# The second feed-forward product in Strassen's form, and lower parts of weights by an accumulating load, in a two-layer encoder trunk

## The chip, the cores and the metric

The kernel runs on one core of one Trainium2 chip. The metric is the device time of one execution in microseconds (us), as a median over runs; smaller is better.

## What is computed

Two layers, each with attention, a recurrent branch and a feed-forward block, over 768 tokens (512 and 256 in two groups) of 1024 features. The change touches the feed-forward block alone:

```python
def encoder_layer(x, l, ...):
...
    x = x + merged @ w_out
    h2 = rmsnorm(x, norm2_g)
    return x + jnp.square(jax.nn.relu(h2 @ w_ff1)) @ w_ff2     # w_ff1 1024 x 4096, w_ff2 4096 x 1024, fp32
```

## The kernel before, in words

**Precision.** Every fp32 operand is split into an upper part (`hi`, rounded to the fp32r type of the matmul) and a lower part `lo = x - hi`. A product is three matmuls: hi x hi, hi x lo, lo x hi. `split` (L203 to L209) makes the two: ACT copies the upper part (L206), DVE subtracts (L209).

**Weights.** `plan` lists every weight tile of 128 x 1024 in the order of use. `wload` (L274) hands out the next and has `prefetch` (L257) prepare the one eight places on: SP loads it into a buffer `raw` or `rw`, ACT and DVE split it into `whi` and `wlo`, of which there are four buffers each. Every engine works in order on its own instructions. PE's order is that of the code; a scheduler sets that of ACT, DVE, POOL and SP.

**Feed-forward.** The 4096 hidden features go in 8 chunks of 512 (L963 on). The features on the partitions are the contraction; tokens are the free dimension, in two halves `TS[0]`, `TS[1]` of 384. In a chunk:

- FF1, `h2 @ w_ff1`, is in the Strassen-Winograd form, seven products q over quarters (two halves of the features, two halves of tokens). Of its weights a1, a2 and b2 are quarters as loaded, P1 to P4 are sums of quarters, made by `ff_operand` on DVE (L235 to L255). A strip is twelve matmuls (4 blocks of the contraction, three each) into a PSUM tile of 128 x 384. `FP` gives the order of the 14 strips as pairs (p, q), p the half of the hidden features. Strips with equal b accumulate in the same tile (L987), `bank[p, b]`.
- After certain strips ACT copies out of PSUM (L996, L998, L1003), DVE combines (L1000, L1004, L1009) and `hidden` follows: DVE takes the positive part times the row scale (L973), ACT squares (L974), `split` makes upper and lower part, 384 wide, into `hs`.
- FF2, `... @ w_ff2`, is plain: four weight tiles of two output blocks jj each, two token halves t, twelve matmuls each in `mm3` (L286 to L288), 16 strips, and DVE adds each tile of 128 x 384 to the residual `xt` (L1024).

So a chunk has 14 x 12 + 16 x 12 = 360 matmuls of 384 columns. PSUM for the block has eight tiles of one bank. In the first chunk of a layer the row scale `rb2` itself is computed after strip (1, 6) by `stats` (matmuls L370 and L371, DVE L320 and L323). In the last chunk each finished residual tile is stored.

Of the kernel before, what the change touches and what calls it, by code (L numbers as in the profile page):

```python
# [79 lines left out]
def trunk_kernel(ctx: ExitStack, tc: tile.TileContext, xT, wqk, wv, wx, wy, wg0, wg1, wa, wr, wo, wf1, wf2,  # L80
                 rgw, vec, rep, rot, out):
# [5 lines left out]
    mp = ctx.enter_context(tc.tile_pool(name="mp", bufs=8))  # L87
# [115 lines left out]
    def split(hi, lo, src, eng="act"):  # L203
# [3 lines left out]
        else:  # L207
# [5 lines left out]
          "wf1": wf1, "wf2": wf2, "rgw": rgw}  # L213
    plan, ready = [], []
    for l in range(DEPTH):
# [14 lines left out]
        for c in range(FF // 512):  # L230
            plan += [("wf1", l, c, x) for x in FW] + [("wf2", l, c * 4 + s) for s in range(4)]
# [24 lines left out]

    def prefetch(upto):  # L257
        while len(ready) < min(upto, len(plan)):
            k = plan[len(ready)]
            if k[0] == "wf1":  # L260
                raw, n = ff_operand(*k[1:]), 1024
# [9 lines left out]
            split(hi, lo, raw)  # L271
# [61 lines left out]
    def squares(xt, g, alloc, before=None):  # L333
# [13 lines left out]
        hi, lo = alloc(n, F32R, "s"), alloc(n, F32R, "s")  # L347
# [33 lines left out]
    def slot(tag, dt=F32, w=T):  # L381
        return mp.tile([P, w], dt, tag=tag, name=nm("s" + tag))
# [4 lines left out]
    def norm1(l, xt, alloc):  # L387
# [23 lines left out]
    nTh, nTl, nss = norm1(0, xt, lambda n, dt, s: slot(gx, dt, n) if s == "s" else e0.tile([P, n], dt, tag="e", name=nm(s)))  # L411
    st0.close()

    for l in range(DEPTH):
# [442 lines left out]
        ppf = pool(ffst, f"pf{l}", bufs=8, space=PSUM)  # L857
# [97 lines left out]


        nss = []
        for off, n in GROUPS:
            nss.append([mp.tile([P, n], F32R, tag=gl, name=nm("s")) for i in range(2)])
            split(*nss[-1], sqa[:, off:off + n])  # L960
        rb2 = cp.tile([P, T], F32, tag="rb", name=nm("rb"), bufs=1)
        NC_ = FF // 512
        for c in range(NC_):  # L963
            last = c == NC_ - 1
            hs = {}

            def hidden(s, t, z, r_):

                for i in range(2):
                    if (s, i) not in hs:  # L970
                        hs[s, i] = slot(gl, F32R) if not last else eslot(F32R) if s < 2 else rslot(F32R)
                hi, lo = (hs[s, i][:, TS[t]] for i in range(2))
                V.scalar_tensor_tensor(out=r_, in0=z, scalar=0.0, in1=rb2[:, TS[t]], op0=ALU.max, op1=ALU.mult)  # L973
                S.activation(r_, r_, AF.Square, scale=0.5)  # L974
                split(hi, lo, r_)
# [141 lines left out]
```

## Time and profile before

| | |
|---|---|
| median of 3 runs | 2671.68 us (2670.53 to 2671.82) |
| the profiled execution | 2671.98 us |
| its span (first to last instruction) | 2670.2 us |
| PE busy, matmuls | 2637.9 us (99%), 16456 |
| PE weight loads | 2491.2 us (93%) |
| DVE busy | 1827.0 us (68%) |
| ACT busy | 1414.1 us (53%) |
| POOL busy | 93.8 us (4%) |

A busy share is the share of the span in which the engine executes something; the engines work side by side and wait for each other by semaphores. The feed-forward block is the stretch from about 839 to 1340 us in layer 0 and the last 500 us in layer 1. PE is the matmul engine TensorE, DVE VectorE, ACT ScalarE, POOL GpSimd, SP SyncE, which here issues loads.

### The profile page before, as it was taken

How to read it: one execution, taken by the hardware profiler on the slowest of the kernel's cores; microseconds unless marked ns; L12 is line 12 of the kernel's file. 1: busy time of each engine (PE TensorE's matmuls, PEld its weight loads, DVE VectorE, ACT ScalarE, POOL GpSimd, SP SyncE). 2: the span in 40 equal slices, each digit the busy share in tenths (PEclk: the TensorE clock that was granted, in tenths of full speed). 3: DMA queues.
4: the chain of work that ended last, by engine and by line, in shares of the span. 5: the costliest groups of instructions: out<-in, count | busy, mean ns of one | idle time of the engine just before them, and what ended most of it. 6: DMA issues, size and time to landing. Idle time of an engine off the chain costs nothing.

```text
span 2670.2 us, 40667 instructions
## 1 busy us (share of the span) xinstructions
PE 2637.9 (99%) x16456; PEld 2491.2 (93%) x16456; DVE 1827.0 (68%) x3222; ACT 1414.1 (53%) x2453; POOL 93.8 (4%) x134
## 2 busy tenths in 40 slices
PE   8999999999999999999999999999999999999999
PEld 8999888888889999999999998888888899999999
DVE  8877873698568666555678788737975686555654
ACT  7787872477435333333467878715683363333332
POOL 0000000000020000000100000000001200000000
PEclk9999999999999999999999999999999999999999
DMA  3111114212331221211221111231223321211112
GB/s 133 54 46 53 50 65 144 66 58 71 121 115 64 71 73 64 71 64 56 100 72 52 42 64 38 92 128 55 69 65 122 115 72 64 72 64 64 64 56 79
DMA packets 57484, 199.33 MB, mean 75 GB/s; under 512 B 7504, under 2 KB 10960, under 8 KB 57296
## 3 DMA queue, kind: packets, MB, share of 16 engines
q1 hardware_dynamic: 48384, 161.50, 18.3%
q0 software_dynamic: 8192, 34.61, 3.6%
q8 instruction: 129, 2.11, 0.3%
q10 hardware_dynamic: 720, 0.62, 0.1%
q14 instruction: 59, 0.48, 0.1%
HBM read 177.83 MB, written 18.87 MB: 74 GB/s over the span
## 4 chain that ended last, share of the span: by engine, by line
PE 85%; DVE 7%; ACT 6%; issue 1%; DMA 0%; DVEq 0%; ACTq 0%
PE d L286 13%; PE d L288 13%; PE d L287 13%; PE d L992 6%; PE d L991 6%; PE d L993 6%; PE d L433 4%; PE d L434 4%; PE d L432 4%; PE s L609 3%; PE d L311 2%; PE d L310 2%; PE d L312 2%; PE d L561 2%; PE d L559 2%; PE d L560 2%
## 5 line engine op out<-in xcount | busy, mean ns | idle before, releaser
L206 ACT ACTIVATE whi<-raw 128x1024 fp32r<-128x1024 f32 (+1 forms) x272 | 280.1, 1031 | 455.3 <-PE d L287 277.5
L209 DVE TENSOR_TENSOR wlo<-raw,whi 128x1024 fp32r<-128x1024 f32 (+1 forms) x272 | 330.2, 1216 | 92.0 <-ACT whi L206 89.5
L286 PE MATMUL d<-sZ,whi 128*128 128x384 f32 (+2 forms) x896 | 300.4, 335 | 0.3 <-DVE rec L379 0.3
L287 PE MATMUL d<-sX,whi 128*128 128x384 f32 (+2 forms) x896 | 300.4, 335 | 0.0
L287 PE MATMUL d<-sZ,whi 128*128 128x384 f32 (+2 forms) x896 | 300.4, 335 | 0.0
L288 PE MATMUL d<-sZ,wlo 128*128 128x384 f32 (+2 forms) x896 | 300.2, 335 | 0.0
L286 PEld LDWEIGHTS d<-sZ,whi 128*128 128x128 f32 x896 | 169.1, 189 | 9.4 <-DVE rec L379 0.5
L288 PEld LDWEIGHTS d<-sZ,wlo 128*128 128x128 f32 x896 | 169.1, 189 | 9.0
L287 PEld LDWEIGHTS d<-sZ,whi 128*128 128x128 f32 x896 | 169.1, 189 | 8.8
L287 PEld LDWEIGHTS d<-sX,whi 128*128 128x128 f32 x896 | 169.1, 189 | 8.8
L206 ACT ACTIVATE whi<-ws 128x1024 fp32r<-128x1024 f32 x48 | 50.9, 1061 | 235.5 <-PE d L287 212.8
L286 PE MATMUL d<-sX,whi 128*128 128x384 f32 (+2 forms) x512 | 171.1, 334 | 0.0
L288 PE MATMUL d<-sX,wlo 128*128 128x384 f32 (+2 forms) x512 | 171.1, 334 | 0.0
L432 PE MATMUL d<-whi,sY 128*128 128x256 f32 x512 | 147.8, 289 | 0.0
L432 PE MATMUL d<-whi,sZ 128*128 128x256 f32 x512 | 147.8, 289 | 0.0
L197 ACT ACTIVATE p<-s,nb,sc 128x512 f32<-128x512 f32 (+1 forms) x192 | 134.5, 703 | 21.8 <-DVE nb L612 20.1
L434 PE MATMUL d<-whi,sZ 128*128 128x256 f32 x512 | 145.3, 284 | 0.0
L433 PE MATMUL d<-wlo,sY 128*128 128x256 f32 x512 | 145.2, 284 | 0.0
L434 PE MATMUL d<-whi,sX 128*128 128x256 f32 x512 | 145.2, 284 | 0.0
L433 PE MATMUL d<-wlo,sZ 128*128 128x256 f32 x512 | 145.1, 283 | 0.0
L1024 DVE TENSOR_TENSOR sZ<-sZ,d 128x384 f32<-128x384 f32 x128 | 69.6, 553 | 109.2 <-PE d L288 109.2
L1024 DVE TENSOR_TENSOR sY<-sY,d 128x384 f32<-128x384 f32 x128 | 69.5, 552 | 92.7 <-PE d L288 92.7
(360 smaller groups left out, 7875.7 us busy)
## 6 DMA issues: line engine op xcount, KB each, us to landing
raw<-wf SPq DMA_DIRECT2D x96, 512.0 KB, 3.2
raw<-wqk SPq DMA_DIRECT2D x32, 512.0 KB, 3.4
raw<-wg SPq DMA_DIRECT2D x32, 512.0 KB, 3.3
rw<-wf SPq DMA_DIRECT2D x32, 512.0 KB, 3.3
raw<-wv SPq DMA_DIRECT2D x16, 512.0 KB, 3.8
raw<-wa SPq DMA_DIRECT2D x16, 512.0 KB, 4.5
raw<-wx SPq DMA_DIRECT2D x16, 512.0 KB, 3.2
raw<-wy SPq DMA_DIRECT2D x16, 512.0 KB, 3.2
```

Source lines behind the costliest of these rows:

```text
L206: S.activation(hi, src, AF.Copy)
L209: V.tensor_tensor(out=lo, in0=src, in1=hi.bitcast(F32), op=ALU.subtract)
L286: PE.matmul(ps, lhsT=wh, rhs=xh, start=(k == 0), stop=False)
L287: PE.matmul(ps, lhsT=wh, rhs=xl, start=False, stop=False)
L288: PE.matmul(ps, lhsT=wl, rhs=xh, start=False, stop=(k == n - 1))
L432: PE.matmul(j, lhsT=xh, rhs=hi[:, kk], start=(k == 0), stop=False)
L433: PE.matmul(j, lhsT=xh, rhs=lo[:, kk], start=False, stop=False)
L434: PE.matmul(j, lhsT=xl, rhs=hi[:, kk], start=False, stop=(k == 7))
L991: PE.matmul(ps, lhsT=hi[:, k], rhs=oh, start=new and k == 0, stop=False, skip_group_check=True)
L992: PE.matmul(ps, lhsT=hi[:, k], rhs=ol, start=False, stop=False, skip_group_check=True)
L993: PE.matmul(ps, lhsT=lo[:, k], rhs=oh, start=False, stop=k == 3, skip_group_check=True)
L1024: V.tensor_tensor(out=xg, in0=xg, in1=ps, op=ALU.add)
```

## The change

**FF2 in Strassen's form.** In all chunks but layer 0's last, FF2 takes seven products too, in the order `FP2 = (1, 2, 6, 5, 3, 7, 4)`, each over all four strips r of a quarter of the output (two blocks of 128) before the next product begins. A strip is six matmuls (2 blocks of the contraction), so a chunk has 7 x 4 x 6 = 168 where 192 stood. The weights are a1, a2, b2 and P1 to P4 again (with other signs), made by `ff_operand`. The hidden tiles `b11, b12, b21, b22` (512 features x 768 tokens, as pairs) are summed on DVE and split 768 wide by `h_split` (L209 on ACT, L212 on DVE), seven times a chunk. DVE adds two finished strips at a time into the residual, 128 x 2 x 384 (L1063), 14 times a chunk.

**Lower parts of plain weights.** For a1, a2 and b2 of both products, six a chunk, DVE's subtraction is gone: ACT writes the upper part (L293) and then minus the upper part into `wlo` (L294), and POOL issues a load of the same weights out of DRAM that adds to what stands in `wlo` (L295).

**PSUM and slots.** For chunks there are four PSUM tiles of two banks in place of eight of one bank; the two halves p of FF1, and two strips r of FF2, lie in one tile. The token tiles come in pairs so that two residual blocks are adjacent. Layer 0's last chunk stays plain (`wf2s`), with two blocks jj in one PSUM tile.

```diff
+FP2 = (1, 2, 6, 5, 3, 7, 4)
+FW2 = {1: "a1", 2: "a2", 6: "P2", 5: "P1", 3: "P4", 7: "P3", 4: "b2"}
...
-    mp = ctx.enter_context(tc.tile_pool(name="mp", bufs=8))
+    mp = ctx.enter_context(tc.tile_pool(name="mp", bufs=4))
...
+    def strassen2(l, c):
+        return l + 1 == DEPTH or c + 1 < FF // 512
...
         for c in range(FF // 512):
-            plan += [("wf1", l, c, x) for x in FW] + [("wf2", l, c * 4 + s) for s in range(4)]
+            plan += [("wf1", l, c, x) for x in FW]
+            plan += [("wf2", l, c, FW2[q]) for q in FP2] if strassen2(l, c) else [("wf2s", l, x) for x in range(4)]
...
-            split(hi, lo, raw)
+            if acc is None:
+                split(hi, lo, raw)
+            else:
+                S.activation(hi, raw, AF.Copy)
+                S.activation(lo, hi.bitcast(F32), AF.Copy, scale=-1.0)
+                G.dma_start(out=lo, in_=acc, accum_op=ALU.add)
...
-        ppf = pool(ffst, f"pf{l}", bufs=8, space=PSUM)
+        st = ExitStack()
+        ppf = pool(st, f"pf{l}", bufs=8, space=PSUM)
...
+        st.close()
+        ppf = pool(ffst, f"pff{l}", bufs=4, space=PSUM)
+        def banks():
+            return ppf.tile([P, 2, 512], F32, tag="d", name=nm("d"))
...
-                if new:
-                    bank[p, b] = ppf.tile([P, TH], F32, tag="d", name=nm("d"))
-                ps = bank[p, b]
+                if b not in bank:
+                    bank[b] = banks()
+                ps = bank[b][:, p, 0:TH]
...
+            def h_split(src, late=False):
+                hi, lo = (eslot(F32R), eslot(F32R)) if late else (slot(gl, F32R), slot(gl, F32R))
+                split(hi, lo, src)
+                return [z.rearrange("p (k t) -> p k t", k=2) for z in (hi, lo)]
+            def two(out, u, v, op):
+                V.tensor_tensor(out=out, in0=u, in1=v, op=op)
+            b11, b12, b22, b21 = (hid[x] for x in ("a0", "a1", "b1", "b0"))
+            if str2:
+                o2 = {1: h_split(b11), 2: h_split(b21)}
+                two(b12, b22, b12, ALU.subtract)
+                two(b11, b12, b11, ALU.add)
+                o2[6] = h_split(b11)
+                xb, yb, zb = {}, {}, {}
+                for q in FP2:
+                    if q == 5:
+                        o2[3] = h_split(b22)
+                        two(b22, b22, b11, ALU.subtract)
+                        o2[5] = h_split(b22)
+                    elif q == 7:
+                        o2[7] = h_split(b12)
+                    elif q == 4:
+                        two(b21, b21, b11, ALU.subtract)
+                        o2[4] = h_split(b21)
+                    hi, lo = (a.rearrange("p (r k c) -> p r k c", r=4, c=P) for a in wload("wf2", l, c, FW2[q]))
+                    oh, ol = o2[q]
+                    bk = {2: yb, 7: zb, 4: zb}.get(q, xb)
+                    for r in range(4):
+                        if r // 2 not in bk:
+                            bk[r // 2] = banks()
+                        ps = bk[r // 2][:, r % 2, 0:TH]
+                        for k in range(2):
+                            PE.matmul(ps, lhsT=hi[:, r, k], rhs=oh[:, k], start=q in (1, 2, 7) and k == 0, stop=False,
+                                      skip_group_check=True)
+                            PE.matmul(ps, lhsT=hi[:, r, k], rhs=ol[:, k], start=False, stop=False, skip_group_check=True)
+                            PE.matmul(ps, lhsT=lo[:, r, k], rhs=oh[:, k], start=False, stop=k == 1, skip_group_check=True)
+                        if r % 2:
...
+                            x_ = xp[r // 2 * 2 + ab][:, :, TS[t]]
+                            two(x_, x_, bk[r // 2][:, :, 0:TH], ALU.add)
```

**Where rows move.** Names in the rows: `d` is a PSUM tile, `sX`, `sY`, `sZ` and `e` are token tiles, the number behind a name tells tiles apart; a wait names the engine or the DMA queue whose semaphore it is. All places are in a middle chunk of layer 1.

PE in FF1, from the end of strip (0, 1) into strip (1, 1), before:

```order
L992 MATMUL d_25876<-sY_22386,whi_25456 128x384
L993 MATMUL d_25876<-sY_22386,wlo_25457 128x384
L991 MATMUL d_25890<-sY_22186,whi_25456 128x384 [waits DVE_49]
L992 MATMUL d_25890<-sY_22186,whi_25456 128x384
L993 MATMUL d_25890<-sY_22186,wlo_25457 128x384
```

and with the change:

```order
L1031 MATMUL d_24601<-sY_22205,whi_24285 128x384
L1032 MATMUL d_24601<-sY_22205,wlo_24286 128x384
L1030 MATMUL d_24601<-sY_22007,whi_24285 128x384 [waits Activation_49]
L1031 MATMUL d_24601<-sY_22007,whi_24285 128x384
L1032 MATMUL d_24601<-sY_22007,wlo_24286 128x384
```

Where strip (1, 1) began in a tile of its own, it now begins in the other half of the tile of (0, 1), and its first matmul has a wait on ACT in place of one on DVE. ACT's instruction is the copy out of that tile (L1035). In the same way strip (1, 6) waits for the copy of (0, 6), L1037, and (0, 4) for that of (1, 7), L1042.

ACT around the copy of (1, 7), the second of the two that were L1003, before:

```order
L1003 ACTIVATE e_25348<-d_25356 128x384 [waits PE_49]
L974 ACTIVATE e_25348<-e_25348 128x384 [waits DVE_49]
L206 ACTIVATE whi_25286<-raw_25284 128x1024 [waits DMAHW2_49,PE_49]
L206 ACTIVATE sX_25500<-e_25348 128x384 [waits Activation_49]
L974 ACTIVATE e_25346<-e_25346 128x384 [waits DVE_49]
L206 ACTIVATE whi_25352<-raw_25350 128x1024 [waits DMAHW4_49,PE_49]
L206 ACTIVATE sX_25520<-e_25346 128x384 [waits Activation_49]
L1003 ACTIVATE e_25348<-d_25370 128x384 [waits PE_49]
```

and with the change (L1042 is the copy, L1015 the Square, L293 and L294 the two parts of a plain weight, L209 an upper part):

```order
L1015 ACTIVATE e_24594<-e_24594 128x384 [waits DVE_49]
L293 ACTIVATE whi_24561<-rw_24553 128x1024 [waits DMAHW1_49,PE_49]
L294 ACTIVATE wlo_24562<-whi_24561 128x1024 [waits DMASW6_49,PE_49,Activation_49]
L293 ACTIVATE whi_24596<-raw_24559 128x1024 [waits DMAHW4_49,PE_49]
L1015 ACTIVATE e_24592<-e_24592 128x384 [waits DVE_49]
L294 ACTIVATE wlo_24597<-whi_24596 128x1024 [waits DMASW5_49,PE_49,Activation_49]
L1042 ACTIVATE e_24594<-d_24601 128x384
L209 ACTIVATE sX_24840<-e_24592 128x768 [waits Activation_49]
L1015 ACTIVATE e_24594<-e_24594 128x384 [waits DVE_49]
```

Behind the first copy stood a Square, an upper part of a weight, an upper part of a hidden tile, a Square, and so on; now two weights with both parts stand there, and the second copy comes after a Square and the second weight's lower part. That second weight's upper part waits for PE: for strip (1, 7), the last user of its buffer.

DVE in FF2, a stretch of the part that prepares the later products (L212 lower parts, L1063 sums and adds out of PSUM, L249 sums of weights), with the change:

```order
L1063 TENSOR_TENSOR e_24593<-e_24594,e_24593 128x768 [waits Activation_49]
L1063 TENSOR_TENSOR sZ_21927<-sZ_21927,d_24857 128x2x384 [waits PE_49]
L212 TENSOR_TENSOR wlo_24693<-ws_24630,whi_24692 128x1024 [waits DMASW0_49,DMASW4_49,DVE_49,DMASW6_49,PE_49,Activation_49]
L1063 TENSOR_TENSOR e_24592<-e_24593,e_24592 128x768 [waits DVE_49]
L1063 TENSOR_TENSOR sZ_21929<-sZ_21929,d_24871 128x2x384
L1063 TENSOR_TENSOR sZ_21927<-sZ_21927,d_24891 128x2x384 [waits DVE_49,PE_49]
L212 TENSOR_TENSOR sX_24848<-e_24592,sX_24848 128x768 [waits Activation_49]
L212 TENSOR_TENSOR wlo_24714<-rw_24555,whi_24713 128x1024 [waits DMASW1_49,PE_49,Activation_49]
L1063 TENSOR_TENSOR sZ_21929<-sZ_21929,d_24905 128x2x384 [waits DVE_49]
L212 TENSOR_TENSOR sX_24950<-e_24594,sX_24950 128x768 [waits Activation_49]
L1063 TENSOR_TENSOR sZ_21928<-sZ_21928,d_24857 128x2x384 [waits PE_49]
```

Before, lower parts of weights (L209) and adds of 384 (L1024) stood here alone. Now lower parts of weights sums, differences of hidden tiles, their lower parts and adds of 2 x 384 alternate; the lower part of the operand of q = 6 is `sX_24848`, that of q = 5 `sX_24954`, which comes five rows further on.

## Rows read from the trace of the kernel before

**Rows 1.** Page parts 1 and 4: busy time of each engine; the chain that ended last:
```profile
PE 2637.9 (99%) x16456; PEld 2491.2 (93%) x16456; DVE 1827.0 (68%) x3222; ACT 1414.1 (53%) x2453; POOL 93.8 (4%) x134
PE 85%; DVE 7%; ACT 6%; issue 1%; DMA 0%; DVEq 0%; ACTq 0%
```

**Rows 2.** Windows, one chunk each: length, busy per engine, clock, DMA share, GB/s:
```profile
1166.84:1229.24 62.40, 62.40 (x362) 62.40 (x361) 37.31 (x55) 21.29 (x33) 0.00 (x0) 1.00 0.21 68
2400.00:2462.40 62.40, 62.40 (x362) 62.40 (x361) 37.33 (x53) 21.30 (x33) 0.00 (x0) 1.00 0.20 68
```

**Rows 3.** Waits of PE: in total us, times, longest us:
```profile
PE t L581 <- DVE q L589: 8.3, 10, 1.8
PE t L632 <- DVE q L589: 3.0, 2, 1.5
```

**Rows 4.** DVE timeline, layer 0, a chunk boundary: start, us, line, op, [idle before]:
```profile
1165.69 1.23 DVE L209 TENSOR_TENSOR wlo<-ws,whi 128x1024 fp32r<-128x1024 f32 x1 [2.98 <-ACT whi L206]
1187.75 1.22 DVE L251 TENSOR_TENSOR rw<-rw,rw 128x1024 f32<-128x1024 f32 x1
1188.88 1.48 DVE L1024 TENSOR_TENSOR sY<-sY,d 128x384 f32<-128x384 f32 x3
1195.93 0.56 DVE L1024 TENSOR_TENSOR sY<-sY,d 128x384 f32<-128x384 f32 x1 [1.53 <-PE d L288]
```

**Rows 5.** ACT timeline, same stretch:
```profile
1164.60 1.06 ACT L206 ACTIVATE whi<-ws 128x1024 fp32r<-128x1024 f32 x1 [1.46 <-PE d L992]
1171.21 1.05 ACT L206 ACTIVATE whi<-raw 128x1024 fp32r<-128x1024 f32 x1
1172.16 0.51 ACT L206 ACTIVATE sZ<-e 128x384 fp32r<-128x384 f32 x1
1172.57 0.51 ACT L974 ACTIVATE e<-e 128x384 f32<-128x384 f32 x1
```

**Rows 6.** Groups by line and form: busy us, mean ns:
```profile
L808 DVE TENSOR_TENSOR ri<-ri,xc 128x768 f32<-128x768 f32 x32 | 30.3, 953 | 4.1 <-ACT ri L197 4.1
L834 ACT ACTIVATE sq<-ri 128x768 f32<-128x768 f32 x32 | 25.4, 830 | 0.0
```

**Rows 7.** Timelines of PE, ACT and DVE, layer 0's first chunk:
```profile
839.33 0.34 PE L991 MATMUL d<-sX,whi 128*128 128x384 f32 x1
846.67 0.85 ACT L996 ACTIVATE e<-d 128x384 f32<-128x384 f32 x2
851.82 0.39 PE L370 MATMUL nps<-s,ones 128*128 128x512 f32 x1
855.28 0.69 DVE L320 SCALAR_TENSOR_TENSOR q<-nps,q 128x512 f32<-128x512 f32 x1
```

**Rows 8.** DMA issues: KB each, us to landing:
```profile
raw<-wf SPq DMA_DIRECT2D x96, 512.0 KB, 3.2
af<-ats POOLq DMA_DIRECT2D x16, 384.0 KB, 4.8
```

**Rows 9.** PE timeline around its attention pauses, and windows there (clock after the busy times):
```profile
1600.57 0.63 PE L581 MATMUL t<-ident,qk 128*128 128x128 f32 x4 [0.75 <-DVE q L589]
1602.97 0.41 PE L581 MATMUL t<-ident,qk 128*128 128x128 f32 x2 [1.77 <-DVE q L589]
...
1603.00:1608.00 5.00, 5.00 (x26) 4.63 (x27) 3.22 (x7) 4.08 (x9) 0.00 (x0) 0.66 0.01 3
1604.00:1605.00 1.00, 1.00 (x7) 1.00 (x7) 0.77 (x2) 0.97 (x2) 0.00 (x0) 0.50 0.00 0
...
1683.51 0.63 PE L632 MATMUL t<-ident,w 128*128 128x128 f32 x4 [1.49 <-DVE q L589]
...
1684.00:1685.00 1.00, 1.00 (x11) 1.00 (x10) 1.00 (x3) 0.97 (x3) 0.00 (x0) 1.00 0.00 0
276.00:277.00 1.00, 1.00 (x6) 1.00 (x6) 0.57 (x2) 0.97 (x2) 0.00 (x0) 0.50 0.00 0
```

**Rows 10.** DVE timeline, the last add of the program:
```profile
2666.68 0.56 DVE L1024 TENSOR_TENSOR sZ<-sZ,d 128x384 f32<-128x384 f32 x1 [1.53 <-PE d L288]
```

More of the change, by code (lines that the diff above doesn't have):

```diff
@@ L379, in scaled, with slot, slots @@
         V.scalar_tensor_tensor(out=out, in0=ps, scalar=-0.5, in1=rb[:, off:off + n], op0=ALU.mult, op1=ALU.mult)
-    def slot(tag, dt=F32, w=T):
-        return mp.tile([P, w], dt, tag=tag, name=nm("s" + tag))
+    spare = {}
+    def slot(tag, dt=F32):
+        if (tag, dt) in spare:
+            return spare.pop((tag, dt))
+        t_ = slots(tag, dt)
+        spare[tag, dt] = t_[:, 1]
+        return t_[:, 0]
+    def slots(tag, dt=F32):
+        return mp.tile([P, 2, T], dt, tag=tag, name=nm("s" + tag))
     def pool(st, name, **kw):
@@ L390, in norm1, with sums @@
         nl = [slot(gl, F32R) for k in range(KT)]
-        ss = []
+        ss, st_ = [], []
+        def sums():
+            if not st_:
+                st_.append(slots(gx, F32R))
+            return st_[0]
         for g in range(2):
@@ L954, in trunk_kernel @@
                 split2(o, k, xt[k + 4][:, TS[o - 2]], gn(k + 4))
[L957 to L960, printed above, removed]
+        st.close()
+        ppf = pool(ffst, f"pff{l}", bufs=4, space=PSUM)
+        def banks():
+            return ppf.tile([P, 2, 512], F32, tag="d", name=nm("d"))
+        sst = slots(gl, F32R)
+        split(sst[:, 0], sst[:, 1], sqa)
         rb2 = cp.tile([P, T], F32, tag="rb", name=nm("rb"), bufs=1)
@@ L963, in trunk_kernel, with hidden @@
         for c in range(NC_):
[L964 to L973, printed above, removed]
+            last, str2 = c == NC_ - 1, strassen2(l, c)
+            hid = {x: eslot() for x in ("a0", "a1", "b1", "b0")}
+            def hidden(x, p, z, r_):
+                V.scalar_tensor_tensor(out=r_, in0=z, scalar=0.0, in1=rb2[:, TS[int(x[1])]], op0=ALU.max, op1=ALU.mult)
                 S.activation(r_, r_, AF.Square, scale=0.5)
-                split(hi, lo, r_)
             ws, bank = {}, {}
-            zz = [eslot() for i in range(4)]
             for i, (p, q) in enumerate(FP):
@@ L1006, in trunk_kernel @@
                 elif q == 4:
-                    hidden(2 * p + 1, 0, ps, y4)
+                    hidden("b0", p, ps, y4)
                 elif q == 3:
                     V.tensor_tensor(out=m16, in0=m16, in1=ps, op=ALU.add)
-                    hidden(2 * p, 1, m16, m16)
+                    hidden("a1", p, m16, m16)
                 if c == 0 and i == 5:
-                    for g_ in range(2):
-                        stats(nss[g_], rb2, None, g_, lambda n, s: mp.tile([P, n], F32, tag=gl, name=nm(s)), ppf, "d")
@@ L1015, in trunk_kernel @@
[L1015 to L1029 removed]
+                    yq = slots(gl)
```

108 lines of the change are left out of this document (61 added, 47 removed).

## The prediction

> **What bounds the kernel now.** I read the page first, then the time by stage, then the waits, then single instructions. The page says that TensorE (PE) is busy 99% of the span and carries 85% of the chain that ended last [rows 1]. That alone does not say what a feed-forward chunk is worth, so I cut one chunk of each layer out of the trace: both last 62.40 us, PE is busy in all of it, DVE in 37.3 us and ACT in 21.3 us [rows 2]. The 360 matmuls of 384 columns of a chunk divide this into 0.1733 us each; a strip of 12 ends every 2.08 us, as an add into the residual shows, 0.55 long after 1.53 of waiting [rows 4]. The list of PE's waits has no feed-forward line at all [rows 3]. So in these stages every matmul costs 0.173 us, and the other engines are free as long as they are never late. The profiled execution took 2671.98 us, 0.3 above the median of 2671.68, and the sum is made against it. Under 0.2% (5 us) a measurement of this kernel can't tell from no change.
>
> **What is removed.** A Strassen chunk does its second product in 7 x 4 strips of 6 matmuls, 168 where 192 stood. 15 of the 16 chunks have it (layer 0's last is plain), so 15 x 24 x 0.1733 = 62.4 us of PE work go, 4.16 a chunk: a chunk of 336 matmuls needs 58.24 us of PE.
>
> **What is added, in prices.** DVE instructions that stand back to back start 0.47 us apart at 384 elements (three in 1.48) and 1.13 apart at 1024 (1187.75 to 1188.88) [rows 4]; at 768, whose duration lies between (0.95, [rows 6]), the same slope gives 0.868. On ACT the pitch is 0.95 at 1024 and 0.41 at 384, the full durations 1.06, 0.83 (768) and 0.51 [rows 5, 6]. From the end of an ACT instruction to the start of the DVE instruction that waited for it pass 0.03 us (1164.60 + 1.06, then 1165.69) [rows 4, 5]; for PE I take 0.06. A reader of a strip starts 0.2 us after PE has issued it, since a matmul takes 0.34 where one is issued every 0.17 [rows 7]. I write F for the moment at which PE has issued the last strip of the first product, FF1. Other numbers of a mid chunk (all but the first and last of a layer have the same order on DVE and ACT) follow from the order tables.
>
> **FF1 gets three waits.** A PSUM tile now holds the two halves p = 0 and 1, and the first matmul of a strip waits for the reader of the other half. (a) Strip (1,1) waits for ACT's copy of (0,1), just finished: 0.2 + 0.5 + 0.06, about 0.75 us. (b) (1,6) waits in the same way for the copy of (0,6): 0.75. (c) (0,4) waits for the copy (L1042) of (1,7), the strip before it. In ACT's queue this copy stands behind an upper part that itself waits for (1,7), a Square and a lower part: 0.02 + 0.95 + 0.41 + 0.95 + 0.5 + 0.06 = 2.9 us. Nothing covers these: PE works in order. Sum 4.4 us.
>
> **FF2 becomes DVE's.** From F - 1.0 on (the upper part of P2's weights waits for strip (1,4), which ends at F - 2.08, and takes 1.06) DVE has no pause until the lower part of q = 5's operand: 22 instructions, of which 7 of 1024 (lower parts of P2, P1, P4, P3, the sum P4, and two sums for the next chunk), 2 of 384 and 13 of 768 (three differences and sums, four lower parts, six adds out of PSUM). 7 x 1.13 + 2 x 0.47 + 13 x 0.868 = 20.2 us, so that operand is there at F + 19.3. PE reaches q = 5 at F + 12.5 without waits; its second matmul needs the lower part, so the product starts in effect at F + 19.2, and 6.7 us are lost, about 2.2 of them already before q = 6. After it the queue keeps up: the adds that free a bank for q = 3 end just ahead of it. A mid chunk thus takes 58.24 + 4.4 + 6.7 = 69.4 us, **7.0 more** than now. The loads are not in the way: the next chunk's second quarter is issued when DVE has used up its predecessor, and lands 3.2 us later [rows 8], as DVE gets there. The lower parts that no longer pass DVE (six a chunk) are what it was spared; without that the stretch would be longer still.
>
> **The other chunks.** In the first chunk of a layer ACT is behind: its copies of (0,1) and (1,1) ran at 846.67, 7.3 us after FF1's start at 839.33 [rows 7]. (1,1) now waits for the first of them: 846.67 + 0.43 + 0.06 less the 841.41 at which (0,1) ends, 5.7 in place of 0.75. The norm's two tiles take two of the four PSUM buffers, so strip (0,2) waits for the reader L320, which ended 855.97, 4.15 after those matmuls began at 851.82 [rows 7]; with ACT's longer order about 5, less 0.7 of PE work: 4.4. So 7.0 + 5.0 + 4.4 = 16.4, twice. Layer 0's plain chunk saves nothing, has the 4.4 of FF1, and in each of its 8 tiles the second half waits for DVE's add of the first: 0.2 + 0.55 + 0.06 = 0.8 at least, 2.1 where weights or norm work stand ahead; 10 in all: 14.4. The very last chunk prepares no successor (two sums fewer, one difference moved ahead): 5.6; its last add is 768 wide, 0.4 longer than the 384 that ends the program now [rows 10], and for a second store behind it I put 0.3. Sum: 2 x 16.4 + 12 x 7.0 + 14.4 + 5.6 + 0.7 = 137.5, that is 2671.98 + 137.5 = 2809.5 with the clock kept.
>
> **The clock.** Per chunk PE now stands still for 2.9 us at (0,4), for 0.6 and 1.6 around one matmul at q = 6, and for 1.9 and 2.6 around one at q = 5. In the trace of before, pauses of 0.75 and 1.77 us with four transposes between them come once in each layer, and both times the granted clock then stands at 0.50, the lower of its two levels; its mean over the 5 us after 1603 is 0.66 [rows 9], so 5 x 0.34 = 1.7 us of work are lost each time. A single pause of 1.49 us comes twice [rows 3] and drops nothing [rows 9]. Bounds per chunk: 0, and 1.7 at (0,4), 1.7 at q = 5 and 0.6 at q = 6 (where DVE sets the end anyway), 4.0. I take 3.2, nearer to the rows that dropped, since the pauses at (0,4) and q = 5 are longer than theirs, but the low stretch may begin in the pause: 15 x 3.2, 1.6 in the plain chunk. **Forecast: 2809.5 + 49.6 = 2859 us.** The Trainium skill, page "TensorE: Matmul & The Clock Gate", section "A second HAM failure mode: psum-queue depth-cycling", says that an engine that idles briefly between matmul groups while it cycles through PSUM keeps falling back to the low clock. By that rule every pause would count, also the 0.75 us of FF1 and 1.49 us, and the time be at the upper bound of 4.0 a chunk, 2809.5 + 15 x 4.0 + 1.7 = 2871 or more; the trace agrees with it at pauses that add up to 2.5 us, not at one of 1.49.
>
> **The accumulating load** is in no row. PE needs its result between 10.4 us (the next chunk's a1, the shortest) and 14 us after ACT's part is done. The nearest rows are plain loads: 3.2 us for 512 KB on SP, 4.8 for 384 KB on POOL [rows 8]. Lower bound 3.2; upper, twice the slowest per byte, 12.8. I take about 6, so no wait; at 12.8 it would cost 2.4 a chunk. The page "DMA: Bandwidth & Descriptors" of the Trainium skill, section "Anatomy of one DMA — SWDGE (gpsimd) path", fits 2.0 us plus the bytes at 436 GB/s, which gives an estimate of 3.2 us for 512 KB; it prices no accumulation, and by it the sum stays as it is. No run here shows it.
>
> **Rivals.** *Waits without the clock*: all of the above, but the clock stays up: 2810 us. For it: the pauses of 1.49 us that dropped nothing, and at q = 6 and q = 5 one matmul that splits them; against: the two that dropped [rows 9]. *Slow accumulation*: a load of 15 us or more holds PE at a1 of each chunk, 16 x 5 or more = 80: 2939 and up. For it: nothing like it was measured; against: DMA engines are a fifth busy [rows 2]. *Faster: the waits don't bind.* The order tables name the engine of a wait, and I read from the operands which instruction is meant. If (0,4) and q = 5 waited for older work, PE would stay the bound with 4.16 us less a chunk: 2672.0 - 62.4 = 2610. It decides at the point where a chunk's waits sum to less than 4.16 us. For it: DVE's sum over the chunk is some 46 us of 58, so on average there is room. Against: the room lies in FF1 and the load in FF2, and the three waits of FF1 alone are above 4.16. Near that point the time would be the same.
>
> **How the numbers follow.** Waits and clock 0.66, waits without clock 0.14, slow accumulation 0.14, faster 0.04, same 0.02. So slower 0.94. The range: its low end is the time without the clock less half of FF1's small waits, should ACT be ahead there (16 x 0.75 = 12): 2797. Its high end takes every pause at its upper bound, 15 x 4.0 + 1.7 = 62, and as much again as one pause in each of the long waits of the first chunks (4 x 1.7 = 7), and 12 for adds out of two banks that no row shows: 2890. It leaves out most of the slow accumulation and the faster case.
>
> **What would show it.** Right: mid chunks of 69 to 73 us; PE waits of some 2.9 us on ACT's L1042 in each chunk and of 1.5 to 3 us on DVE's lower parts (L212) at q = 6 and q = 5; DVE without a pause for 20 us after F; a granted clock below 1 in the feed-forward slices; stages before them unchanged. Wrong: chunks near 58 us with a busy PE, or PE waiting for the accumulating load.

## The result, and the profile after

| | before | with the change |
|---|---|---|
| median of the runs | 2671.47 us (2670.53 to 2671.82, 4 runs) | 2870.49 us (2868.39 to 2876.89, 4 runs) |
| span of the profiled execution | 2670.2 us | 2866.6 us |
| mean granted clock | 0.998 | 0.975 |

The change is slower: ratio 1.075, 95% interval 1.0731 to 1.0768. The prediction was 2859 us, range 2797 to 2890.

The page, parts 1 and 4, of the changed kernel, against [rows 1]:

```profile
PE 2672.5 (93%) x16096; PEld 2486.3 (87%) x16096; DVE 1994.8 (70%) x3243; ACT 1582.6 (55%) x2570; POOL 177.0 (6%) x227
PE 75%; DVE 13%; ACT 8%; issue 3%; DMA 1%; ACTq 0%; DVEq 0%
```

360 matmuls are gone (16456 to 16096), and still PE is busy for longer, since part of its work ran at the lower clock. Its share of the chain fell from 85 to 75%, that of DVE rose from 7 to 13%.

Windows of the changed kernel, against [rows 2]: FF1 and FF2 of one middle chunk of layer 0, FF1 of one of layer 1, and FF2 of the chunk in layer 0 just before (length; busy time of PE, weight loads, DVE, ACT, POOL; clock, DMA share, GB/s):

```profile
995.69:1031.22 35.53, 31.50 (x169) 30.54 (x169) 15.54 (x21) 18.55 (x26) 3.50 (x4) 0.95 0.53 119
1031.22:1069.78 38.56, 33.54 (x169) 32.15 (x169) 33.01 (x36) 13.94 (x16) 1.75 (x2) 0.91 0.34 82
2499.52:2533.52 34.00, 29.96 (x169) 29.00 (x169) 15.54 (x21) 18.56 (x26) 3.50 (x4) 1.00 0.55 125
959.00:995.69 36.69, 32.03 (x169) 30.64 (x169) 32.90 (x36) 13.94 (x16) 1.75 (x2) 0.95 0.35 86
```

The chunk is 74.1 us long where it was 62.4; the twelve middle chunks last 73.0 on average. FF1 has the same 168 matmuls as before and takes 35.5 us (29.1 before, 168 x 0.1733). FF2 has 24 fewer, 29.1 us of work, and takes 38.6; DVE works in it for 33.0 us, more than PE's own 29.1. FF1 of the third row is 34.0 us long with the clock at 1.00: the same waits without the low stretch, the time at a clock of 0.50. The fourth is an FF2 of 36.7 us with the clock low for a shorter time. FF2 takes 36.4 to 37.1 us in five of the middle chunks and 38.3 to 38.7 in seven.

The list of PE's waits, against [rows 3], where it had no feed-forward line (in total, times, longest, us):

```profile
PE d L1030 <- ACT e L1042: 44.5, 16, 2.9
PE d L1093 <- DVE sX L212: 22.6, 16, 2.8
PE d L1093 <- DVE sZ L212: 19.3, 14, 1.8
PE d L1091 <- ACT sX L209: 16.3, 16, 1.7
PE d L1030 <- ACT e L1035: 15.5, 16, 3.7
PE d L1091 <- ACT sZ L209: 14.3, 14, 1.7
PE d L1030 <- ACT e L1037: 9.3, 16, 0.6
PE t L620 <- DVE q L628: 8.4, 10, 1.8
PE d L310 <- DVE sY L1115: 8.2, 8, 1.8
```

Seven of the nine lines are the three waits of FF1 (L1035, L1037, L1042) and two products of FF2 (L1091, the first matmul of a strip, waits for an upper part; L1093, the second, for a lower part); L310 is the plain chunk. L620 is the attention wait that headed [rows 3] with 8.3 us; the others of before stand below, nearly unchanged. No line names an accumulating load. In time, PE in the chunk of the first two windows (start, us, engine, line, operation [idle before <- releaser]):

```profile
998.52 0.44 PE L1030 MATMUL d<-sX,whi 128*128 128x384 f32 x1 [0.58 <-ACT e L1035]
...
1021.24 0.46 PE L1030 MATMUL d<-e,whi 128*128 128x384 f32 x1 [2.87 <-ACT e L1042]
...
1040.26 0.45 PE L1091 MATMUL d<-sZ,whi 128*128 128x384 f32 x1 [0.35 <-ACT sZ L209]
...
1041.98 0.69 PE L1093 MATMUL d<-sZ,whi 128*128 128x384 f32 x1 [1.27 <-DVE sZ L212]
...
1049.51 0.45 PE L1091 MATMUL d<-sZ,whi 128*128 128x384 f32 x1 [1.70 <-ACT sZ L209]
...
1051.64 0.45 PE L1093 MATMUL d<-sZ,whi 128*128 128x384 f32 x1 [1.69 <-DVE sZ L212]
```

0.58 at (1, 1), the same at (1, 6), 2.87 at (0, 4); then 0.35 and 1.27 around one matmul at q = 6, 1.70 and 1.69 around one at q = 5. The matmul after a pause takes 0.44 us in place of 0.34.

DVE in the same FF2, against [rows 4]:

```profile
1034.64 0.95 DVE L212 TENSOR_TENSOR sZ<-e,sZ 128x768 fp32r<-128x768 f32 x1
1035.51 0.95 DVE L1063 TENSOR_TENSOR e<-e,e 128x768 f32<-128x768 f32 x1
...
1046.63 0.95 DVE L1063 TENSOR_TENSOR e<-e,e 128x768 f32<-128x768 f32 x1
1047.50 1.22 DVE L249 TENSOR_TENSOR ws<-rw,raw 128x1024 f32<-128x1024 f32 x1
...
1049.50 1.22 DVE L249 TENSOR_TENSOR ws<-ws,rw 128x1024 f32<-128x1024 f32 x1
1050.63 0.95 DVE L212 TENSOR_TENSOR sZ<-e,sZ 128x768 fp32r<-128x768 f32 x1
```

The pitch at 768 elements is 0.87 us (1034.64 to 1035.51). Between 1030.27 and 1054 DVE pauses once, for 0.96 us, behind PE. The difference for q = 5 is at 1046.63; two sums for the next chunk (L249) and, at 1048.63, an add into the residual stand between it and its lower part at 1050.63, and PE's matmul at 1051.64 waits for that. The wait before it, the 1.70 that ended at 1049.51, is in part ACT's:

```profile
1047.67 1.06 ACT L293 ACTIVATE whi<-raw 128x1024 fp32r<-128x1024 f32 x1 [5.78 <-PE d L1093]
1048.63 0.83 ACT L209 ACTIVATE sZ<-e 128x768 fp32r<-128x768 f32 x1
```

The difference was done at 1047.58, but its upper part (L209) stood in ACT's queue behind a weight copy (L293) that had waited for PE to be done with its buffer in q = 6. DVE's lower part comes later still, so DVE sets when the product gets going.

The clock around those pauses, windows against [rows 9]:

```profile
998.00:1000.00 2.00, 1.48 (x8) 1.48 (x9) 0.00 (x0) 0.47 (x1) 0.88 (x1) 1.00 1.07 266
1022.00:1023.00 1.00, 1.00 (x5) 1.00 (x4) 1.00 (x2) 0.52 (x1) 0.00 (x0) 0.50 0.97 184
1049.00:1054.00 5.00, 2.81 (x10) 2.55 (x11) 5.00 (x6) 2.14 (x3) 0.88 (x1) 0.82 0.68 153
2499.52:2550.70 51.18, 43.79 (x242) 41.44 (x241) 32.19 (x40) 26.23 (x35) 3.50 (x4) 1.00 0.43 105
```

After the pause of 0.58 the clock is 1.00. After 2.87 it is 0.50 for 3 us in one chunk (1022). In another of layer 1 it is 1.00 from the start of FF1, past a pause of 2.88 at (0, 4), to the start of q = 5 (2499.52 on). Around q = 5 of the first chunk (1049 on) its mean is 0.82 over 5 us. PE at q = 5 of the other one, whose FF2 began at 2533.53:

```profile
2550.24 0.44 PE L1091 MATMUL d<-sX,whi 128*128 128x384 f32 x1 [1.70 <-ACT sX L209]
...
2553.51 0.69 PE L1093 MATMUL d<-sX,whi 128*128 128x384 f32 x1 [2.83 <-DVE sX L212]
```

It comes to q = 5 16.7 us after the start of FF2, where the first chunk, with a low stretch at q = 6, comes after 18.3; but it waits longer there, and the second matmul starts after 20.0 and 20.4 us.

The first chunk of layer 0, PE at the first matmul of FF1 and at (1, 1), against [rows 7]:

```profile
840.42 0.41 PE L1030 MATMUL d<-sX,whi 128*128 128x384 f32 x1 [1.18 <-DVE sY L982]
...
846.47 0.44 PE L1030 MATMUL d<-sX,whi 128*128 128x384 f32 x1 [3.70 <-ACT e L1035]
```

And the accumulating load, against [rows 8] (KB each, median us to landing):

```profile
wlo<-wf POOLq DMA_DIRECT2D x93, 512.0 KB, 6.8
```

### The profile page after: what moved, and what is told of

It is laid out like the page before. It is cut to its first block, busy times and chain, and to the rows that moved or that the text cites. A ratio compares the mean times of both kernels' runs of the same rounds, so it can differ in the third digit from the quotient of the medians.

```text
span 2866.6 us, 40417 instructions
## 1 busy us (share of the span) xinstructions
PE 2672.5 (93%) x16096; PEld 2486.3 (87%) x16096; DVE 1994.8 (70%) x3243; ACT 1582.6 (55%) x2570; POOL 177.0 (6%) x227
## 4 chain that ended last, share of the span: by engine, by line
PE 75%; DVE 13%; ACT 8%; issue 3%; DMA 1%; ACTq 0%; DVEq 0%
PE d L1030 6%; PE d L310 6%; PE d L311 6%; PE d L312 6%; PE d L1031 6%; PE d L1032 6%; PE d L1093 4%; PE d L1094 4%; PE d L1091 4%; PE d L471 3%; PE d L472 3%; PE d L473 3%; PE s L648 2%; DVE wlo L212 2%; PE d L335 2%
## 5 line engine op out<-in xcount | busy, mean ns | idle before, releaser
L209 ACT ACTIVATE whi<-raw 128x1024 fp32r<-128x1024 f32 (+1 forms) x180 | 183.5, 1021 | 321.3 <-PE d L311 166.3
L212 DVE TENSOR_TENSOR wlo<-raw,whi 128x1024 fp32r<-128x1024 f32 (+1 forms) x180 | 218.8, 1219 | 43.6 <-ACT whi L209 42.4
L1030 PE MATMUL d<-e,whi 128*128 128x384 f32 x384 | 137.0, 357 | 53.8 <-ACT e L1042 44.5
L1093 PE MATMUL d<-sX,whi 128*128 128x384 f32 x448 | 159.5, 356 | 22.6 <-DVE sX L212 22.6
L1091 PE MATMUL d<-sX,whi 128*128 128x384 f32 x448 | 158.4, 354 | 16.3 <-ACT sX L209 16.3
L209 ACT ACTIVATE whi<-ws 128x1024 fp32r<-128x1024 f32 x93 | 98.6, 1060 | 122.2 <-PE d L1093 71.4
L293 ACT ACTIVATE whi<-raw 128x1024 fp32r<-128x1024 f32 x62 | 65.4, 1055 | 172.1 <-PE d L1093 127.1
L1093 PE MATMUL d<-sZ,whi 128*128 128x384 f32 x392 | 140.4, 358 | 19.3 <-DVE sZ L212 19.3
L1094 PE MATMUL d<-sX,wlo 128*128 128x384 f32 x448 | 157.0, 350 | 0.0
L295 POOL DMA_DIRECT2D wlo<-wf x93 | 81.5, 876 | 1161.2 <-ACT wlo L294 1092.0
L1091 PE MATMUL d<-sZ,whi 128*128 128x384 f32 x392 | 139.2, 355 | 14.3 <-ACT sZ L209 14.3
L310 PE MATMUL d<-sZ,whi 128*128 128x512 f32 (+1 forms) x448 | 150.8, 337 | 0.3 <-DVE rec L402 0.3
L311 PE MATMUL d<-sZ,whi 128*128 128x512 f32 (+1 forms) x448 | 150.7, 336 | 0.0
L311 PE MATMUL d<-sX,whi 128*128 128x512 f32 (+1 forms) x448 | 150.7, 336 | 0.0
L312 PE MATMUL d<-sZ,wlo 128*128 128x512 f32 (+1 forms) x448 | 150.6, 336 | 0.0
L1015 ACT ACTIVATE e<-e 128x384 f32<-128x384 f32 x128 | 66.6, 520 | 145.8 <-DVE e L1014 145.7
```

The source lines that it names most:

```text
L209: S.activation(hi, src, AF.Copy)
L212: V.tensor_tensor(out=lo, in0=src, in1=hi.bitcast(F32), op=ALU.subtract)
L310: PE.matmul(ps, lhsT=wh, rhs=xh, start=(k == 0), stop=False)
L311: PE.matmul(ps, lhsT=wh, rhs=xl, start=False, stop=False)
L312: PE.matmul(ps, lhsT=wl, rhs=xh, start=False, stop=(k == n - 1))
L1030: PE.matmul(ps, lhsT=hi[:, k], rhs=oh, start=new and k == 0, stop=False, skip_group_check=True)
```

## The experiments

Two questions: is each wait of FF1 a price of its own, or does DVE's work set the chunk in any case; and what is the accumulating load worth?

**e1: FF1's halves apart.**

```diff
-                if b not in bank:
-                    bank[b] = banks()
-                ps = bank[b][:, p, 0:TH]
+                if b == 1:
...
+                else:
+                    if (p, b) not in bank:
+                        bank[p, b] = one()
+                    ps = bank[p, b][:, 0:TH]
```

> The changed kernel, but the two halves p of FF1 lie in PSUM tiles of their own again (four tiles of one bank, and two of two banks for b = 1 and for products 1, 6, 5, 3); products 2, 7 and 4 then add 384 at a time, 6 DVE instructions more a chunk, 6 x (2 x 0.47 - 0.87) = 0.4 us. Theory (the waits of FF1 are false ones between halves of a tile, each with its own price): PE's waits on the ACT copies L1035, L1037, L1042 go, 69 us in the trace of the change, with about 1.5 us of low clock behind the one of 2.9 us in 13 chunks and the 8 us of half waits in the plain chunk; 69 + 20 + 8 less 16 x 0.4: some 90 less, 2780 us, FF1 of a mid chunk 29.1 in place of 35.5 us, FF2 still 36 to 39 us. Rival (DVE's total work sets the length of a chunk and PE only waits for it earlier or later): FF1 shrinks but FF2 grows by nearly as much, 2840 us or more.

Measured: 2777.66 us, ratio to before 1.040 (1.0384 to 1.0415), 93 us under the change. Windows of FF1 and FF2 of a middle chunk of layer 1:

```profile
2500.32:2529.44 29.12, 29.12 (x169) 29.12 (x169) 15.19 (x22) 18.06 (x26) 3.50 (x4) 1.00 0.62 144
2529.44:2568.53 39.09, 31.92 (x169) 30.56 (x169) 33.79 (x41) 14.33 (x16) 1.75 (x2) 0.91 0.32 82
```

FF1 is back at 29.1 us with the clock at 1.00, PE's waits there are gone, and they were false: nothing of the values needed them. FF2 is 39.1 us, and 39.4 on average over the middle chunks where the changed kernel had 37.7, so the rival has 1.7 us a chunk. PE in that FF2, at q = 5:

```profile
2549.42 0.69 PE L1104 MATMUL dd<-sX,whi 128*128 128x384 f32 x1 [5.54 <-ACT sX L209]
```

With FF1 quick, most of the lost time stands in this one wait.

**e2: sums of weights on POOL.**

```diff
-            V.tensor_tensor(out=fw[out], in0=fw[u], in1=fw[v], op=op)
+            G.tensor_tensor(out=fw[out], in0=fw[u], in1=fw[v], op=op)
```

> The changed kernel, but the sums of weight quarters (P1 to P4 of both products, eight a chunk) are made on POOL in place of DVE. Theory (FF2 waits because DVE's queue is too long up to the operand of q = 5): two of the sums for the next chunk and one for P4 leave that stretch, which in the new order is 15.2 us of back-to-back work from P1's lower part on where it was 17.4 us with them; the wait before q = 5 (1.70 and 1.69 in a mid chunk) falls by 2.3 us and with it perhaps the low clock there, 1.5: 15 x 2.3 to 15 x 3.8, that is 2813 to 2836 us; FF1's waits of 0.58, 0.58 and 2.87 us stay. Rival (a wait on POOL takes its place: a sum of 1024 takes about 2.8 us there by the 2.1 us of its 768-wide sums, three stand in one queue with the issues of the accumulating loads): PE waits on POOL's sums or on late lower parts, and the time stays within 10 us of 2870 or is above it.

Measured: 2994.57 us, ratio 1.121 (1.1194 to 1.1228), 124 us over the change. The number is the rival's, the mechanism is not. PE's list names no POOL and no lower part of a weight in these chunks. DVE is busy 1999.0 us with 3119 instructions where it was busy 1994.8 with 3243. DVE in two places:

```profile
2559.08 6.57 DVE L212 TENSOR_TENSOR sX<-e,sX 128x768 fp32r<-128x768 f32 x3 [0.69 <-ACT sX L209]
...
2639.31 0.95 DVE L1063 TENSOR_TENSOR sZ<-sZ,d 128x768 f32<-128x768 f32 x1 [1.21 <-PE d L1094]
```

and POOL at the same times:

```profile
2558.55 2.36 POOL L249 TENSOR_TENSOR ws<-ws,rw 128x1024 f32<-128x1024 f32 x1
2560.86 3.10 POOL L249 TENSOR_TENSOR rw<-rw,rw 128x1024 f32<-128x1024 f32 x1
...
2637.32 3.02 POOL L249 TENSOR_TENSOR ws<-rw,raw 128x1024 f32<-128x1024 f32 x1 [14.64 <-DVE sZ L1063]
```

Three lower parts of 768 took 6.57 us beside two sums of POOL, where three take 2.7 without. An add that reads PSUM (2639.31) took its usual 0.95 inside a sum of POOL. The group of those lower parts, first in e2, then in the changed kernel (busy us, mean ns):

```profile
L212 DVE TENSOR_TENSOR sX<-e,sX 128x768 fp32r<-128x768 f32 x56 | 94.7, 1713 | 6.2 <-ACT sX L209 6.2
```

```profile
L212 DVE TENSOR_TENSOR sX<-e,sX 128x768 fp32r<-128x768 f32 x56 | 53.2, 952 | 0.8 <-ACT sX L209 0.6
```

1.71 us on average against 0.95; in e2 the median is still 0.95 and the longest 3.12. So an instruction of DVE with both operands in SBUF is held up while POOL runs one, and taking 2.3 us out of DVE's queue gave it more than that back. The Trainium skill says so: "GPSIMD Engine Reference", section "1. Specifications", puts contention with DVE instructions that have two SBUF inputs under POOL's SBUF interface. The rows agree, and the expectation of e2 had left it out. The rival of a late accumulating load isn't seen. With the longer waits the clock fell too: its mean over the run is 0.947 in place of 0.975, by which at most 87 of the 124 us are the clock's (an estimate from the two means).

**e3: no accumulating load in the changed kernel.**

```diff
-            if acc is None:
+            if True:
                 split(hi, lo, raw)
```

> The changed kernel, but all lower parts of weights are DVE subtractions again, no accumulating load. Theory: the load is hidden and spares DVE six instructions a chunk, of which in this order one stands before the operand of q = 5 (1.1 us), the others where DVE has pauses; on ACT the minus-copies L294 go, and the copy L1042 of strip (1,7) comes 1.4 us sooner, so that the wait at (0,4) is 1.5 in place of 2.9 us, perhaps too short to lower the clock (1.5 more). Sum: 15 x 1.1 - 16 x 1.4 - 13 x 0 to 1.5 = -6 to -25, that is 2845 to 2865 us. Rival 1 (DVE's total sets the chunk): 15 x 6 x 1.13 = 102 more, 2970 us. Rival 2 (the accumulating loads themselves hold PE): over 40 us less, below 2830 us.

Measured: 2878.31 us, ratio 1.077 (1.0757 to 1.0789), 8 us over the change, with intervals that overlap, and above the expected 2845 to 2865. PE's waits:

```profile
PE d L1093 <- DVE sX L212: 35.2, 16, 4.7
PE d L1093 <- DVE sZ L212: 32.4, 14, 3.9
PE d L1030 <- ACT e L1042: 30.1, 16, 1.9
```

The wait at (0, 4) fell from 44.5 to 30.1 us in total, as expected, and was short enough to spare the clock in some chunks (FF1 33.1 in place of 34.6 us in 6 of the 13 middle and last ones). But the lower parts in FF2 cost 67.6 in place of 41.9 us: 1.7 us a chunk where 1.1 was expected. In the changed kernel the load is worth little either way, against both rivals.

**e4: the accumulating load in the kernel before.**

```diff
-            split(hi, lo, raw)
+            if acc is None:
+                split(hi, lo, raw)
+            else:
+                S.activation(hi, raw, AF.Copy)
+                S.activation(lo, hi.bitcast(F32), AF.Copy, scale=-1.0)
+                G.dma_start(out=lo, in_=acc, accum_op=ALU.add)
```

> The kernel before, with plain second products, but the lower parts of its seven plain weight tiles a chunk by the accumulating load: one part of the change alone. Theory: PE was the bound with all else covered, DVE loses 7 x 1.13 us a chunk that nobody waited for, ACT gains 7 x 0.95, and the load lands in some 7 us where its user is 12 us or more away: no difference, 2668 to 2676 us. Rival (the load is late for the operands of FF1, which PE uses up in 4.2 us each): 16 chunks x 1 us or more, above 2690 us.

Measured: 2783.98 us, ratio 1.042 (1.0406 to 1.0440), 112 us over the kernel before. The theory fell, and the waits are not the rival's. PE at the start of FF2 of a middle chunk:

```profile
2465.06 0.44 PE L295 MATMUL d<-sX,whi 128*128 128x384 f32 x1 [2.43 <-ACT sX L206]
...
2467.64 0.69 PE L296 MATMUL d<-sX,whi 128*128 128x384 f32 x1 [2.14 <-DVE sX L209]
```

It waits for ACT's upper and DVE's lower part of a hidden tile, and FF1 is 29.1 us as before. In the last strips of FF1 ACT now has four copies of 1024 where two stood, ahead of the last hidden tiles. e8 takes that alone.

**e8: ACT's second copy alone, in the kernel before.**

```diff
-            split(hi, lo, raw)
+            S.activation(hi, raw, AF.Copy)
+            if k[0] == "wf2" or k[0] == "wf1" and k[3] in ("a1", "a2", "b2"):
+                S.activation(lo, hi.bitcast(F32), AF.Copy, scale=-1.0)
+            V.tensor_tensor(out=lo, in0=raw, in1=hi.bitcast(F32), op=ALU.subtract)
```

> The kernel before with ACT's second copy (minus the upper part) for the seven plain weight tiles of a chunk put in front of DVE's subtraction, which stays and overwrites it: no accumulating load, the same values. It tells apart why the accumulating load in the kernel before cost 112 us. Theory (ACT's copies stand in front of the upper parts of the last hidden tiles, so the first strips of FF2 wait for them): nearly the same loss without any load, 2740 to 2800 us, PE waiting at the start of FF2 on ACT's and DVE's parts of the hidden tiles. Rival (the loads, by their traffic or by POOL, hold ACT, DVE or PE back): 2671 to 2685 us.

Measured: 2754.56 us, ratio 1.031 (1.0292 to 1.0326), 83 us over the kernel before, with no load at all. PE's waits, two of three lines at the start of FF2:

```profile
PE d L289 <- ACT sZ L206: 20.9, 7, 3.0
PE d L289 <- ACT sX L206: 20.9, 7, 3.0
```

So 83 of the 112 us are the copies in ACT's queue, with the low clock that their waits bring. DVE's subtraction has to wait for the second copy too, but PE's list has under 2 us for DVE's lower parts. The other 29 aren't taken apart by a run. In e4 PE waits 31.7 us for DVE's lower parts of hidden tiles (L296), since two sums of weights, held up by a load, had got in front of them (2464.64 and 2465.89), and the mean clock of the run is 0.985 where e8 has 0.991.

**e5: FF2's DVE work in another order.**

```diff
                 for q in FP2:
-                    if q == 5:
+                    if q == 2:
                         o2[3] = h_split(b22)
                         two(b22, b22, b11, ALU.subtract)
                         o2[5] = h_split(b22)
-                    elif q == 7:
+                    elif q == 3:
                         o2[7] = h_split(b12)
-                    elif q == 4:
+                    if q == 3:
                         two(b21, b21, b11, ALU.subtract)
                         o2[4] = h_split(b21)
...
+                                later += [(x_[:, i], bk[r - 1 + i][:, 0:TH]) for i in range(2)]
...
+                        if r == 3 and q not in (2, 6) or r % 2 and q in (7, 4):
+                            for u, v in later:
+                                two(u, u, v, ALU.add)
...
```

> e1 (FF1's halves apart) with FF2's DVE work in another order, none of it removed: the operands of q = 3 and 5 are made before q = 2 in the program text, those of q = 7 and 4 before q = 3, and the adds of q = 2 into the residual come after q = 5. Theory (the place of q = 5's operand in DVE's queue sets FF2): its lower part, which came 18.7 us after the start of P1's lower part in e1's order, comes after 15.0; FF2 of a mid chunk 34 to 36 in place of 39.2 us, 15 x 3.7 to 15 x 5.4 (with the low clock of that pause gone too) less: 2697 to 2722 us. Rival (DVE's sum of work in FF2 sets it, in whatever order): the wait moves to q = 3, 7 or 4, and the time is 2765 us or more.

Measured: 2717.48 us, ratio 1.017 (1.0153 to 1.0187), 60 us under e1, in the upper part of the expected range. FF2 of a middle chunk:

```profile
2485.94:2521.56 35.62, 31.77 (x169) 30.59 (x169) 33.38 (x41) 14.06 (x16) 1.74 (x2) 0.95 0.36 90
```

35.6 us where e1 had 39.1, with DVE busy for nearly the same time (33.4 against 33.8). The place in the queue set it, not the sum of the work.

**e6: weights prepared three places ahead.**

```diff
-        prefetch(i + 1 + AHEAD)
+        prefetch(i + 1 + (3 if key[0][:2] == "wf" else AHEAD))
...
-        return fw[x], fw.get("d" + x)
+        return fw[x], None if x == "a1" else fw.get("d" + x)
...
-                    for g, (off, n) in enumerate(GROUPS):
-                        stats(...)
+                    np2 = banks()
+                    for g, (off, n) in enumerate(GROUPS):
+                        for k in range(2):
+                            PE.matmul(np2[:, g, 0:n], lhsT=ones, rhs=sst[:, k, off:off + n], start=k == 0, stop=k == 1)
...
```

> e5, and weights of the feed-forward block are prepared three places ahead in place of eight (so the three sums for the next chunk leave the stretch before q = 5), a1's lower part is a DVE subtraction again (its accumulating load would now be too near its use), and both groups' norm sums of a layer's first chunk share one PSUM tile. Theory: q = 6's operand is ready 8.6 us after the end of FF1 (PE is there at 8.3), q = 5's and the adds that free its bank after 14.3 (PE at 13.1): FF2 31 to 32 us, a chunk 60 to 61.5, less than the 62.4 of the kernel before; in 15 chunks 14 to 36 us gained, some 8 given back in first and plain chunks: 2645 to 2668 us, faster than both kernels. Rival (a late load or lower part takes the place, since everything is prepared later): PE waits on an accumulating load or on a lower part of a weight in each chunk, 2690 us or more.

Measured: 2650.85 us (2650.34 to 2651.51), ratio 0.9922 (0.9908 to 0.9937): 21 us (0.8%) faster than the kernel before, 220 faster than the change. FF1 and FF2 of a middle chunk, and the longest of PE's waits in it (one line for each layer):

```profile
2402.80:2431.98 29.18, 29.18 (x169) 29.07 (x169) 19.14 (x25) 17.62 (x25) 2.62 (x3) 1.00 0.57 144
2431.98:2463.29 31.31, 29.65 (x170) 29.04 (x169) 31.07 (x41) 13.00 (x15) 0.87 (x1) 1.00 0.27 68
```

```profile
PE dd L1109 <- DVE sZ L1076: 12.5, 8, 1.6
```

A chunk of 60.5 us, the clock at 1.00, DVE at 50.2 of the 60.5 us. Three edits came at once here. By place, some 12 of the 67 us under e5 are in FF1 of the two first chunks (36.8 and 37.1 us in e5, 30.7 and 31.1 here), where the norm sums now share a tile; most of the rest is some 3.8 us in each middle chunk. A wait of 1.6 us is left in FF2, for the add that frees the bank before q = 5.

**e7: e6 without accumulating loads.** The edit is that of e3, on e6.

> e6 without any accumulating load: all lower parts by DVE, four more subtractions a chunk (4.5 us), four copies fewer on ACT. Theory: with q = 5's operand at the same place in DVE's order (14.3 us after FF1) the load is worth little: within 15 us of e6. Rival (DVE's total, now some 53 of 60 us a chunk, sets the length): above e6 by up to 15 x 4.5 = 68 us.

Measured: 2655.40 us, ratio 0.9939 (0.9924 to 0.9954). 4.6 us above e6, intervals overlapping: the load is worth 0 to 5 us of the gain.

## Why the prediction was right, and where not

**The waits of FF1** came in the three places and at nearly the sizes that were put: 0.58, 0.58 and 2.87 us for 0.75, 0.75 and 2.9. (The 0.75 was counted from the issue of the last matmul, 0.17 us before the end from which a pause is listed, so it is met.) FF1 without the low clock is 34.0, 4.9 over the 29.1 of before where 4.4 was put; the pauses listed are 4.0, and the rest is the restart behind each (0.44 in place of 0.34, and the last matmul before it running out). e1 shows that they are the shared tile's: taking it apart gained 93 us, low clock and all.

**FF2 is DVE's**: shown by the back-to-back rows, by e5, which moved the loss by order alone, and by e6. 6.7 us were put, of them 2.2 before q = 6 and 4.5 at q = 5. In the chunk of layer 1 whose clock stayed up until then, 1.6 and 4.5 are listed (1.70 and 2.83); in the one of layer 0, with a low stretch at q = 6, 1.6 and 3.4. From the second matmul of q = 5 on, 16.6 us remain where the clock stays up. Two of the middle chunks have no low stretch before that matmul, and in them it starts 20.0 and 19.6 us after the start of FF2. So FF2 without the clock is about 36.4 us, 7.3 over its work of 29.1, an estimate from these rows.

**The clock** was priced a little too high, and in part in the wrong place. 3.2 us a chunk were put, between 0 and 4.0. By the granted clock the low stretches take 3.4 us of work out of a middle chunk (seven of twelve) or 5.1 (five), but not all of that costs time. At (0, 4) it does: FF1 is 35.6 us with a low stretch and 34.0 without. At q = 6 the pauses of 0.35 and 1.27 lowered the clock in ten of twelve middle chunks, and there the reading that "DVE sets the end anyway" held: PE comes 1.6 us later to q = 5, but its second matmul there starts 19.8 to 20.5 us after the start of FF2, against 20.0 and 19.6 in the other two. At q = 5 seven of twelve chunks have a low stretch, and their FF2 is longer by 1.9 us on average. Taken together, and with only two chunks to go by at q = 6, a middle chunk without the low clock would last about 34.0 + 36.4 = 70.4 us; it lasts 73.0, so the clock costs about 2.6. The waits cost 8.0 where 7.0 was put, and the clock 2.6 where 3.2 was put: the agreement in the sum is partly two errors against each other.

| | put | measured |
|---|---|---|
| twelve middle chunks, each over 62.4 | 7.0 + 3.2 | 8.0 + 2.6 (73.0 us) |
| the two first chunks, each | 16.4 + 3.2 | 19.9 and 20.8 |
| layer 0's plain chunk | 14.4 + 1.6 | 16.0 (78.45 against 62.40) |
| the last chunk | 5.6 + 3.2 | 9.1 |
| after the last matmul | 0.7 | 0.9 |
| before the first strip of FF1, twice | 0 | 1.1 |
| sum | 187 | 196 |

In the first chunk (1, 1) waited 3.70 us where 5.7 was put, (0, 2) 3.65 where 4.4 was, and the granted clock took up to 6.8 and 8.5 us of work where 3.2 was put. The line of the table on the first strip was not seen ahead: FF1's first matmul into the new tiles of two banks waits 1.18 us for DVE's last reader (L982) of the tiles that stood there. In e1, where FF1 begins with tiles of one bank, PE's list has no such wait.

**The rule on pauses** of the Trainium skill ("TensorE: Matmul & The Clock Gate", section "A second HAM failure mode: psum-queue depth-cycling"), taken as "every pause counts", was to give 2871 us or more, and the kernel took 2870.5. The trace does not bear the rule out in that form: pauses of 0.58 us never lowered the clock here, one of 2.87 did in 11 of 13 chunks and did not in two, and a middle chunk paid about 2.6 us for the clock and not 4.0. That the number came nearest is luck: the waits were longer than the sum behind it had them.

**The accumulating load** landed in 6.8 us where about 6 was taken, and PE never waited for it. Its price isn't there: it is ACT's second copy, which stands in the queue before the copy of (1, 7). The prediction had that copy in the 2.9 us of (0, 4), but called the load a relief; e3 and e7 show that relief for DVE and load for ACT about cancel, and e4 and e8 that where DVE had room it only costs. The upper bound of 12.8 took 4.8 us for 384 KB as the slowest plain load; the trace of before has eight of 384 KB on POOL with a median of 7.1 us and eight with 7.5.

**The rivals.** Waits without the clock: shown wrong by the rows at 0.50. Slow accumulation: 6.8 us, not 15. The waits not binding: wrong, PE's list has them. Of the signs put ahead two came in part: middle chunks last 71.9 to 74.2 us, five of twelve more than the 73 named, and DVE's stretch after F has one pause, of 0.96 us.

## What to carry to other kernels

Cutting the bound engine's work is worth nothing until the waits it creates are cheaper than the cut: here 4.2 us a chunk were bought with three false waits in FF1 and a queue of DVE work in FF2. Before two results share a tile, ask who reads the one half while the other is written, and what stands in that reader's queue ahead of it. When an engine's queue, and not its total, is late, reorder it first (operands that PE waits for ahead of adds and of work for later): e5 and e6 got 127 us, nearly all of it from that and with hardly an instruction removed, and only then did the smaller product show its gain.

## What the runs showed of the hardware that was not expected

POOL's sums hold DVE up: 768-wide lower parts of DVE with both operands in SBUF took 1.71 us on average, with POOL's sums beside them, and 0.95 without; a DVE add with one operand in PSUM took 0.95 inside a POOL sum. An accumulating load of 512 KB from DRAM into SBUF took 6.8 us where a plain one took 3.6 to 3.7 in the same run; the first was issued by POOL and the second by SP, and no run tells that apart from the accumulation. The same pause of PE (2.87 us) lowered the clock to 0.50 for some 3 us in 11 chunks of 13 and left it at 1.00 in two; what tells them apart was not found.
